# A decoder step in split fp32: first sums on GpSimd, norms in column groups inside the scans, the last norm's tiles regrouped

## The chip, the core and the metric

The kernel runs on one core of one Trainium2 chip. The metric is the device time of one execution in microseconds, the median of several runs. The engines are TensorE (PE in the profile; its weight loads PEld), VectorE (DVE), ScalarE (ACT), GpSimd (POOL) and SyncE (SP, which issues most DMAs). Each works through its own list in order and waits for the others by semaphores.

## What is computed

One inference step of a hybrid decoder layer, for a prompt of 16 + 1024 tokens and 8 decode samples, width 1024, in fp32:

```
h += 0.5 * swiglu(rmsnorm(h, n1), w1g, w1u, w1d)          # FFN1, inner width 2816
u  = rmsnorm(h, nm) @ w_in                                # q, f, v, g of 4 HGRN2 heads; z, x, B, C, dt of Mamba-2
# HGRN2 head:  S_t = diag(f_t) S_{t-1} + k_t v_t^T,  o_t = S_t^T q_t;  rmsnorm(o) * hg_norm * silu(g)
# Mamba-2:     h_t = exp(dt A) h_{t-1} + dt x B^T,   y = h C + D x;    grouped rmsnorm(y * silu(z)) * ssm_norm
h += concat(hgrn_out, ssm_out) @ w_out
h += 0.5 * swiglu(rmsnorm(h, n2), w2g, w2u, w2d)          # FFN2
y  = rmsnorm(h, norm_final)
```

The outputs are y for prompt and samples and the new recurrent states.

## The kernel before

Channels lie on the 128 partitions, tokens along the free axis: 1048 tokens (1032 after the scans, where the 16 meta tokens are dropped). A product of the large matrices is made in split precision: each operand is the sum of a high part (a cast, ScalarE) and a low part (a subtraction, VectorE), and three matmuls (lines 163, 164, 165) add up in one PSUM bank.

**FFNs.** Each pair of output blocks is made by seven block products in place of eight (Winograd's form of Strassen's scheme), whose operands are sums of blocks: of weights (`Left.sum_`, line 460; high part `hi` 464, low part `lo` 468) and of activations (`Blocks.sum_`, line 343; `cast` 348, `low` 354). `first1` is written for the first pair of FFN1: while the input arrives by DMA in token tiles, `x.place` transposes and scales them for the first pair of blocks, and `x.place_k` (lines 994 to 997) does the rest, channel block by channel block. `before(S, i, ...)` puts work ahead of step i of the product list. The order on TensorE, VectorE, ScalarE and SyncE is that of the code; the order on GpSimd is chosen by a scheduler. GpSimd builds masks at the start (lines 884 to 931) and does little else.

**Scans.** `ssm_scan` runs over nine chunks (the last has 16 tokens), then `hgrn_scan` four times, one head each. The projections that later heads need are cut into small steps; `fill(n)` issues n of them on TensorE between the small matmuls of a scan, so that TensorE has work while VectorE and ScalarE prepare the next level. `hgrn_scan` goes through levels m = 1, 2, 4, ... 64; at each it takes one of the `jobs` handed to it (the norm of the head before). At levels 1 and 32 `samples` loads four decode states by SyncE and updates them on ScalarE (line 1488) and VectorE (1489); after the levels eight one-column matmuls (line 1630), with the 128 x 128 states as weights, read them out. The norms (`hgrn_out`, line 1648, and `ssm_norm`, line 1396) square, sum over partitions by a matmul with a matrix of ones, which leaves the sum on all 128 partitions, and take the inverse root of 1032 columns in `rstd_wide` (ScalarE logarithm and exponential behind a table load, three VectorE steps, lines 203 to 205). The norm of Mamba group 0 runs between heads 0 and 1. Here only TensorE's order is that of the code.

**The end.** In the last `down` of FFN2, `Final` normalises 128 tokens at a time (transposes, line 1703; sum of squares; scale, line 1717), at given steps of the product list, and `LastFinal` takes the last 264 tokens as three tiles of 88 in three parts: transposes at line 1729, ScalarE squares (1735) and VectorE multiplications by the norm's weights (1736). Line 763 adds each finished product to the residual and frees its PSUM bank.

Of the kernel before, what the change touches and what calls it, by code (L numbers as in the profile page):

```python
# [12 lines left out]
AF = mybir.ActivationFunctionType  # L13
# [10 lines left out]
NS = 8  # L24
# [165 lines left out]
def rstd_wide(K, v, r, after):  # L190

    nc = K.nc
    with K.tc.issue_after(after.ins):
        ld = nc.scalar.preload_act_table_set("natural_log_exp_and_others")
    with K.tc.issue_after(ld.ins):
        n = v.shape[1] // 2
        parts = [(v[:, s : s + n], r[:, s : s + n]) for s in (0, n)]
        for vp, rp in parts:
            nc.scalar.activation(rp, vp, AF.Ln)
        for vp, rp in parts:  # L200
            nc.scalar.activation(rp, rp, AF.Exp, scale=-0.5, bias=K.lna)
    return [
        lambda: nc.vector.tensor_mul(v, v, r),
        lambda: nc.vector.scalar_tensor_tensor(v, v, -1.0, r, ALU.mult, ALU.mult),
        lambda: nc.vector.scalar_tensor_tensor(r, v, 3.0 * 2.0 ** (-2.0 / 3.0), r, ALU.add, ALU.mult),
    ]
# [112 lines left out]
class Blocks:  # L319
# [19 lines left out]
    def sum_(self, p):  # L339
        x, y = {5: (7, 1), 6: (3, 5), 7: (3, 7), 4: (2, 6)}[p]  # L340
        x, y = self.b[x], self.b[y]
        t = self.b[p] if p == 7 else self.new(p)
        self.K.nc.vector.tensor_sub(t, x, y)  # L343
# [99 lines left out]
class Left:  # L443
# [12 lines left out]
    def sum_(self, p):  # L456
# [3 lines left out]
        self.K.nc.vector.tensor_tensor(self.raw[p], self.raw[x], self.raw[y], op)  # L460
# [737 lines left out]
def ssm_scan(K, a, o, fill):  # L1198
# [45 lines left out]
    def back(c, hT):  # L1244
# [4 lines left out]
        if c > 0:  # L1249
# [3 lines left out]
            nc.vector.tensor_mul(ec[:, :, :n], pi.rearrange("p (j t) -> p j t", j=4)[:, :, :n], ec[:, :, :n])  # L1253
        py = K.psm()
# [3 lines left out]
        pyv = py.rearrange("p (j t) -> p j t", j=4)  # L1258
        ps = K.psm()
# [124 lines left out]
def ssm_norm(K, g, tag, fill):  # L1384
# [7 lines left out]
    fill(10)  # L1392
    for c0, w in CHUNKS_O:
        cs = slice(c0 - NM, c0 - NM + w)
        ps = K.psm()[:, :w]
        nc.tensor.matmul(ps, K.ones[1], v[:, cs], start=True, stop=True)
# [720 lines left out]
```

## Time and profile before

| | |
|---|---|
| median of 3 runs | 1979.36 us (1977.38 to 1979.84) |
| the profiled execution: its own time, its span | 1983.28 us, 1981.5 us |
| mean granted TensorE clock | 0.991 |
| TensorE, VectorE, ScalarE, GpSimd busy | 98%, 73%, 42%, 4% |
| the largest lines | 163, 164, 165 (split products): 1310.8, 1300.4, 1297.5 us, overlapping |
| DMA | 258.45 MB, mean 130 GB/s |

The span runs from the first to the last instruction; times on the trace count from its start. Busy times of TensorE's lines overlap, since matmuls are pipelined. The stages lie about so: start 0 to 60 us, FFN1 to 850, projections and scans to 1240, output projection and FFN2 to the end.

### The profile page before, as it was taken

The page shows a single profiled execution, that of the slowest core. Times are in us where ns is not written, and L with a number is a line of the kernel's source. Part 1 is how long each engine was busy: PE and PEld are TensorE (multiplying, and loading weights), DVE is VectorE, ACT ScalarE, POOL GpSimd, SP SyncE. Part 2 cuts the span into 40 slices and gives each one's busy share as a digit, 9 for nine tenths or more (in the row PEclk, how much of TensorE's full clock was granted, in tenths as well). Part 3 has the DMA queues.
Part 4 walks back from the last instruction along what each step waited for, and adds up shares of the span by engine and source line. Part 5 has one row for each costly group of instructions (what it writes and reads, how often), then busy time and mean ns, then how long its engine had stood idle before and what let it go on. Part 6 is the DMA issues. An engine that isn't in the chain of part 4 may idle for free.

```text
span 1981.5 us, 40896 instructions
## 1 busy us (share of the span) xinstructions
PE 1937.6 (98%) x16687; PEld 1900.4 (96%) x16687; DVE 1455.1 (73%) x2515; ACT 835.4 (42%) x1587; POOL 85.7 (4%) x135
## 2 busy tenths in 40 slices
PE   7999999999999999999999999999999999999997
PEld 6999999999999999998989999999999999999997
DVE  7777777778688776575665567987777777768974
ACT  7522222224534655465544445742222222354352
POOL 4000000000000410000000002200000000000000
PEclk9999999999999999999999999999999999999999
DMA  7233242335976542232442254224232423487851
GB/s 219 78 100 98 82 129 82 112 83 155 295 246 223 175 133 60 55 102 63 131 121 67 78 167 141 71 87 117 85 109 81 127 83 113 152 245 237 270 179 67
DMA packets 323876, 258.45 MB, mean 130 GB/s; under 512 B 17568, under 2 KB 299424, under 8 KB 323680
## 3 DMA queue, kind: packets, MB, share of 16 engines
q1 hardware_dynamic: 323448, 255.79, 42.6%
q8 instruction: 132, 2.16, 0.5%
q14 instruction: 56, 0.46, 0.1%
q0 software_dynamic: 224, 0.04, 0.0%
q10 hardware_dynamic: 16, 0.00, 0.0%
HBM read 190.79 MB, written 65.05 MB: 129 GB/s over the span
## 4 chain that ended last, share of the span: by engine, by line
PE 84%; DVE 9%; DMA 2%; issue 2%; ACT 2%; SPq 0%; POOL 0%; DVEq 0%; ACTq 0%; POOLq 0%
PE acc L163 26%; PE acc L165 26%; PE acc L164 26%; DVE u L354 1%; DVE ws L468 1%; PE mis L1540 1%; DMA r<-in_w_ffn_up_dram 1%; DMA u<-hd 1%; DVE u L677 1%; DVE ws L739 1%; DVE u L343 0%; PE mis L1261 0%; DVE r L460 0%; PE mis L1600 0%; DVE t L548 0%
## 5 line engine op out<-in xcount | busy, mean ns | idle before, releaser
L163 PE MATMUL acc<-u,ws 128*128 128x258 f32 (+4 forms) x4482 | 1310.8, 293 | 8.4 <-DVE t L562 2.7
L164 PE MATMUL acc<-u,ws 128*128 128x258 f32 (+4 forms) x4482 | 1300.4, 290 | 3.3 <-DVE u L354 1.8
L165 PE MATMUL acc<-u,ws 128*128 128x258 f32 (+4 forms) x4482 | 1297.5, 290 | 3.4 <-DVE ws L468 3.3
L163 PEld LDWEIGHTS acc<-u,ws 128*128 128x128 f32 x4482 | 849.2, 190 | 13.6 <-issue 5.1
L164 PEld LDWEIGHTS acc<-u,ws 128*128 128x128 f32 x4482 | 851.6, 190 | 6.1 <-DVE u L354 2.8
L165 PEld LDWEIGHTS acc<-u,ws 128*128 128x128 f32 x4482 | 849.0, 189 | 5.3 <-DVE ws L468 4.9
L468 DVE TENSOR_TENSOR ws<-r,ws 128x512 fp32r<-128x512 f32 x308 | 212.8, 692 | 78.8 <-ACT ws L464 78.8
L464 ACT CAST ws<-r 128x512 fp32r<-128x512 f32 x308 | 173.8, 615 | 5.0 <-DVE r L460 4.8
L583 ACT ACTIVATE t<-t 128x524 f32<-128x524 f32 (+1 forms) x47 | 29.9, 640 | 299.6 <-DVE t L548 299.6
L460 DVE TENSOR_TENSOR r<-r,r 128x512 f32<-128x512 f32 x176 | 121.1, 690 | 8.3 <-DMA r<-in_w_ffn_up_dram 6.5
L560 ACT ACTIVATE t<-t 128x516 f32<-128x516 f32 (+1 forms) x41 | 26.2, 639 | 200.3 <-DVE t L548 200.3
L677 DVE TENSOR_TENSOR u<-u,u 128x1048 fp32r<-128x1048 f32 (+3 forms) x84 | 97.2, 1159 | 10.2 <-ACT u L673 9.4
L232 POOL TENSOR_TENSOR t<-t,t 128x262 f32<-128x262 f32 (+1 forms) x56 | 57.5, 1036 | 814.9 <-ACT t L231 811.8
L548 DVE TENSOR_TENSOR t<-t,u 128x524 f32<-128x524 f32 (+1 forms) x135 | 90.4, 698 | 2.8
L158 DVE TENSOR_TENSOR ws<-r,ws 128x512 fp32r<-128x512 f32 x88 | 60.9, 702 | 40.0 <-ACT ws L157 39.5
L734 ACT CAST ws<-u 128x512 fp32r<-128x512 f32 (+1 forms) x72 | 42.1, 585 | 99.9 <-DVE u L729 91.6
L673 ACT CAST u<-u 128x1048 fp32r<-128x1048 f32 (+3 forms) x84 | 82.8, 988 | 1.3 <-DMA u<-hd 1.3
L763 DVE SCALAR_TENSOR_TENSOR s<-acc,s 128x524 f32<-128x524 f32 (+3 forms) x86 | 53.8, 649 | 33.8 <-PE acc L165 33.5
L739 DVE TENSOR_TENSOR ws<-r,ws 128x512 fp32r<-128x512 f32 (+1 forms) x84 | 56.3, 681 | 29.8 <-ACT ws L734 29.5
L734 ACT CAST ws<-r 128x512 fp32r<-128x512 f32 (+1 forms) x84 | 47.5, 582 | 65.9 <-DVE r L729 39.7
L553 ACT COPY t<-acc 128x524 f32<-128x524 f32 (+3 forms) x46 | 26.4, 574 | 103.5 <-PE acc L165 103.5
L157 ACT CAST ws<-r 128x512 fp32r<-128x512 f32 x88 | 53.6, 617 | 34.5 <-PE acc L165 31.1
(393 smaller groups left out, 1875.2 us busy)
## 6 DMA issues: line engine op xcount, KB each, us to landing
r<-in_w_ffn_down_dram SPq DMA_DIRECT2D x128, 256.0 KB
hd<-s SPq DMA_DIRECT2D x93, 258.0 KB
r<-in_w_ffn_gate_dram SPq DMA_DIRECT2D x88, 256.0 KB
r<-in_w_ffn_up_dram SPq DMA_DIRECT2D x88, 256.0 KB
hd<-s SPq DMA_DIRECT2D x77, 262.0 KB
u<-hd SPq DMA_DIRECT2D x36, 516.0 KB
u<-hd SPq DMA_DIRECT2D x28, 524.0 KB
r<-in_w_in_dram SPq DMA_DIRECT2D x56, 256.0 KB
```

Of the source, the lines that this page charges most:

```text
L158: self.nc.vector.tensor_sub(lo, src, hi.bitcast(F32))
L163: mm(ps, whi, xhi, start=first, stop=False, skip_group_check=more)
L164: mm(ps, whi, xlo, start=False, stop=False, skip_group_check=more)
L165: mm(ps, wlo, xhi, start=False, stop=last, skip_group_check=more)
L460: self.K.nc.vector.tensor_tensor(self.raw[p], self.raw[x], self.raw[y], op)
L464: self.K.nc.scalar.copy(self.w[p][:, : self.n * P], self.raw[p])
L468: self.K.nc.vector.tensor_sub(t[:, 512 : 512 + w], self.raw[p], t[:, :w].bitcast(F32))
L548: nc.vector.tensor_mul(t, t if src is None else src, spread.lanes(i, cs))
L673: K.nc.scalar.copy(hi, lo.bitcast(F32))
L677: K.nc.vector.tensor_sub(lo, lo.bitcast(F32), hi.bitcast(F32))
L734: nc.scalar.copy(w[p, j, g][:, : n * P], src)
L739: nc.vector.tensor_sub(t[:, 512 : 512 + n * P], box[0], t[:, : n * P].bitcast(F32))
```

## The change

The order rows below are an engine's instructions in program order, with output, input and shape and what is waited for; numbers tell buffers of one name apart.

**First pair of FFN1.** The four sums of weights (products 5, 6, 7, 3) and three of the sums of operands (5, 6, 4 of the second half) are issued on GpSimd. The low parts of product 1 stand ahead of input tile 3. On GpSimd the sums (L478 of weights, L361 of operands; the lines of after stand 18 further down here) come behind the masks:

```order
L914 AFFINE_SELECT mf_8712<-ones_83 128x64 [waits Pool_49]
L915 AFFINE_SELECT mf_8712<-mf_8712 128x64 [waits Pool_49]
L918 CAST mask_8715<-mf_8712 32x16 [waits Pool_49]
L918 CAST mask_8715<-mf_8712 32x16 x3
L478 TENSOR_TENSOR r_239<-r_147,r_149 128x512 [waits DMAHW2_49,DMAHW1_49,Pool_49]
L478 TENSOR_TENSOR r_241<-r_239,r_139 128x512 [waits DMAHW5_49,Pool_49]
L478 TENSOR_TENSOR r_147<-r_139,r_147 128x512
L478 TENSOR_TENSOR r_244<-r_145,r_241 128x512 [waits DMAHW0_49,Pool_49]
L361 TENSOR_TENSOR u_468<-u_328,u_324 128x1048 [waits DVE_49]
```

The seven sums are new there; before, L232 (now L250) followed the last mask. On ScalarE this is the place of product 5 before (L464 is the cast of a sum of weights, L996 and L997 copy a placed input tile out of PSUM):

```order
L553 COPY t_297<-acc_284 128x262 [waits PE_49]
L348 CAST u_299<-u_282 128x1048 [waits DVE_49]
L464 CAST ws_303<-r_301 128x512 [waits DVE_49]
L996 ACTIVATE u_319<-mis_314,col_100 128x262 [waits PE_49]
L997 COPY u_321<-mis_314 128x262
L996 ACTIVATE u_323<-mis_314,col_100 128x250
L997 COPY u_325<-mis_314 128x250
L557 COPY t_339<-acc_284 128x262 [waits PE_49]
```

and now, with L482 as that cast and L1014 and L1015 as the copies:

```order
L571 COPY t_304<-acc_291 128x262 [waits PE_49]
L366 CAST u_306<-u_289 128x1048 [waits DVE_49]
L482 CAST ws_308<-r_239 128x512 [waits Pool_49]
L1014 ACTIVATE u_324<-mis_319,col_100 128x262 [waits PE_49]
L1015 COPY u_326<-mis_319 128x262
L1014 ACTIVATE u_328<-mis_319,col_100 128x250
L1015 COPY u_330<-mis_319 128x250
L575 COPY t_344<-acc_291 128x262 [waits PE_49]
```

The rows are the same; the cast now waits for GpSimd, and the copies stand behind it as they did.

**Scans.** Two `fill(2)` stand between the small matmuls of Mamba's last chunk. `rstd_wide` becomes `Rms`: four matmuls with 32 columns of ones put the sums of a quarter of the tokens each on 32 partitions, so that root and steps work on 258 columns; `part(i)` brings a quarter back to 128 partitions by a matmul with one row. The norm of group 0 becomes a list of jobs inside head 1's scan. Decode states are loaded at levels 1 and 8 and updated at 4 and 64; their readout has 32 columns of weights, mostly zeros, with the states as moving operand, then a ScalarE copy and two four-column matmuls. On TensorE, the end of group 0's norm and the start of head 1 before (L163 to L165 are projection steps, L1396 the norm, L1465 the transposes of head 1):

```order
L163 MATMUL acc_11867<-u_8344,ws_11525 128x344
L164 MATMUL acc_11867<-u_8352,ws_11525 128x344
L165 MATMUL acc_11867<-u_8344,ws_11525 128x344
L1396 MATMUL mis_11883<-s_11846,ones_83 128x344 [waits DVE_49,PE_49]
L1396 MATMUL mis_11886<-s_11846,ones_83 128x344
L1396 MATMUL mis_11889<-s_11846,ones_83 128x344
L163 MATMUL acc_11867<-u_8345,ws_11525 128x344
...
L163 MATMUL acc_11926<-u_8340,ws_11802 128x350 [waits Activation_49]
L164 MATMUL acc_11926<-u_8348,ws_11802 128x350
L165 MATMUL acc_11926<-u_8340,ws_11802 128x350
L1465 MATMUL mis_11933<-ident,u_11067 128x128 x4
```

and the same norm now (L1541 and L1570 are products of head 1's first two levels, L203 the matmuls of `root`):

```order
L164 MATMUL acc_11856<-u_8351,ws_11504 128x344
L165 MATMUL acc_11856<-u_8343,ws_11504 128x344
L1541 MATMUL mis_11904<-u_10571,u_10726 32x32 [waits DVE_49]
L1541 MATMUL mis_11904<-u_10571,u_10726 32x32 x31
L1542 MATMUL mis_11903<-u_10571,u_10726 16x16 [waits Activation_49]
L1570 MATMUL mis_11938<-s_11899,u_10726 32x16 [waits DVE_49,Activation_49]
L1570 MATMUL mis_11938<-s_11899,u_10726 32x16 x31
L1582 MATMUL mis_11903<-s_11899,u_10726 16x8
L203 MATMUL mis_11984<-s_11841,ones_83 32x258 [waits Activation_49]
L203 MATMUL mis_11984<-s_11841,ones_83 32x258 x3
L163 MATMUL acc_11856<-u_8344,ws_11509 128x344
```

The norm's matmuls moved from ahead of head 1 to behind its second level, and there are four of 258 columns for three of 344.

**The end.** The last three `Final`s run at steps closer together, one with banks of the accumulators' pool; `LastFinal` has tiles of 128, 128 and 8 tokens, its first multiplications go to a ScalarE copy and GpSimd, and the second part's square is one instruction of 384 columns into a tile of its own.

```diff
-def rstd_wide(K, v, r, after):
...
+class Rms:
...
+    def root(self):
+        K, w = self.K, self.w
+        nc = K.nc
+        ps = K.psm()[:, :w]
+        for i in range(4):
+            nc.tensor.matmul(ps[32 * i : 32 * i + 32], K.ones[1][:, :32], self.v[:, i * w : i * w + w], start=True, stop=True)
+        self.r, self.q = K.t(w), K.t(w)
+        an = nc.scalar.activation(self.q, ps, AF.Identity, scale=self.scale, bias=K.eps)
+        with K.tc.issue_after(an.ins):
+            ld = nc.scalar.preload_act_table_set("natural_log_exp_and_others")
+        with K.tc.issue_after(ld.ins):
+            nc.scalar.activation(self.r, self.q, AF.Ln)
+            nc.scalar.activation(self.r, self.r, AF.Exp, scale=-0.5, bias=K.lna)
+    def newton(self):
+        nc, q, r = self.K.nc, self.q, self.r
+        nc.vector.tensor_mul(q, q, r)
+        nc.vector.scalar_tensor_tensor(q, q, -1.0, r, ALU.mult, ALU.mult)
+        nc.vector.scalar_tensor_tensor(r, q, 3.0 * 2.0 ** (-2.0 / 3.0), r, ALU.add, ALU.mult)
+    def part(self, i):
+        K, w = self.K, self.w
+        ps = K.psm()[:, :w]
+        K.nc.tensor.matmul(ps, K.ones[1][32 * i : 32 * i + 1], self.r[32 * i : 32 * i + 1], start=True, stop=True)
+        return ps, slice(i * w, i * w + w)
...
-    def sum_(self, p):
+    def sum_(self, p, pool=False):
...
-        self.K.nc.vector.tensor_sub(t, x, y)
+        (self.K.nc.gpsimd if pool else self.K.nc.vector).tensor_sub(t, x, y)
...
-        self.K.nc.vector.tensor_tensor(self.raw[p], self.raw[x], self.raw[y], op)
+        (self.K.nc.gpsimd if pool else self.K.nc.vector).tensor_tensor(self.raw[p], self.raw[x], self.raw[y], op)
...
+        if n < P:
+            fill(2)
         py = K.psm()
...
         pyv = py.rearrange("p (j t) -> p j t", j=4)
+        if n < P:
+            fill(2)
         ps = K.psm()
...
-    fill(10)
-    for c0, w in CHUNKS_O:
-        cs = slice(c0 - NM, c0 - NM + w)
-        ps = K.psm()[:, :w]
-        nc.tensor.matmul(ps, K.ones[1], v[:, cs], start=True, stop=True)
-        an = nc.scalar.activation(v[:, cs], ps, AF.Identity, scale=1.0 / 256, bias=K.eps)
-    for step in rstd_wide(K, v, r, an):
-        step()
-    for i, y in enumerate((ya, yb)):
+    rms = Rms(K, v, 1.0 / 256)
+    def spread(i):
+        ps, cs = rms.part(i)
+        nc.scalar.copy(r[:, cs], ps)
+    def scale(i, y):
         nc.vector.scalar_tensor_tensor(y, y, K.pc["ssm_norm"][:, 2 * g + i : 2 * g + i + 1], r, ALU.mult, ALU.mult)
+    def end():
+        scale(1, yb)
+        then()
+    return [rms.root, lambda: None, rms.newton, lambda: (spread(0), spread(1)), lambda: (spread(2), spread(3)), lambda: scale(0, ya), end]
...
-        if m in (1, 32):
-            samples({1: 0, 32: 4}[m])
+        if m in (1, 8):
+            samples_load({1: 0, 8: 4}[m])
         if jobs:
             jobs.pop(0)()
             fill(2)
+        if m in (4, 64):
+            samples({4: 0, 64: 4}[m])
...
+    qz = K.t(32 * NS).rearrange("p (b i) -> p b i", b=NS)
+    nc.gpsimd.memset(qz, 0.0)
+    nc.scalar.copy(qz[:, :, 0], qs[:, :NS])
     fill(6)
+    pr = K.psm()
+    for b in range(NS):
+        nc.tensor.matmul(pr[32 * (b % 4) : 32 * (b % 4) + 32, b // 4 * P : b // 4 * P + P], qz[:, b], states[b // 4 * 4][:, b % 4], start=True, stop=True)
+    rows = K.t(2 * P)
+    nc.scalar.copy(rows, pr[:, : 2 * P])
+    fill(1)
...
-    for b in range(NS):
-        nc.tensor.matmul(po8[:, 16 + b : 17 + b], states[b // 4 * 4][:, b % 4], qs[:, b : b + 1], start=True, stop=True)
+    for i in range(2):
+        nc.tensor.matmul(po8[:, 16 + 4 * i : 20 + 4 * i], rows[:, i * P : i * P + P], K.ident[:, 0:P:32], start=True, stop=True)
...
+    def gate(i):
+        ps, cs = rms.part(i)
+        nc.vector.tensor_mul(g[:, cs], g[:, cs], ps)
+    def end():
+        gate(3)
         then()
-    jobs = [root, None, None, None, gate]
-    return [lambda i=i: jobs[i]() for i in range(5)]
+    return [rms.root, lambda: None, rms.newton, lambda: (gate(0), gate(1)), lambda: (gate(2), end())]
...
-            ps = K.psm()
+            ps = self.bank()
...
+        self.tiles = [(t0 + c, min(P, n - c)) for c in range(0, n, P)]
...
+            K.nc.scalar.activation(yt[:n, 512:], ps[:n], AF.Square, accum_out=self.st[:n, 0, j : j + 1])
+            K.nc.scalar.copy(yt[:n, :512], ps[:n])
+            K.nc.gpsimd.tensor_mul(yt[:n, :512], yt[:n, :512], self.nf[0][:n, :512])
...
+            K.nc.scalar.activation(junk[:n], ps[:n, : 3 * P], AF.Square, accum_out=st[:n, 1, j : j + 1])
+            for c0, c1, f0 in ((0, 256, 512), (256, 384, 896)):
+                K.nc.vector.tensor_mul(yt[:n, f0 : f0 + c1 - c0], ps[:n, c0:c1], self.nf[0][:n, f0 : f0 + c1 - c0])
...
+        o.low(1)
+        w.lo(1)
+        for p in (5, 6, 7, 3):
+            w.sum_(p, True)
         scaled, raw3 = x.place(3)
         K.keep_clock(4)
         scaled(0)
-        o.low(1)
         scaled(1)
-        w.lo(1)
         w.hi(2)
...
-        before(S, 1, (o.cast, 5), (w.sum_, 5), (w.hi, 5), (o.sum_, 6), (x.store, 0), (columns,), (x.place_k, 0))
-        before(S, 2, (o.low, 5), (o.cast, 6), (w.lo, 5), (w.sum_, 6), (w.hi, 6), (x.place_k, 1))
-        before(S, 3, (o.low, 6), (o.sum_, 7), (w.lo, 6), (o.cast, 7), (w.sum_, 7), (w.sum_, 3), (w.hi, 7), (x.place_k, 2))
+        before(S, 1, (o.cast, 5), (w.hi, 5), (o.sum_, 6), (x.store, 0), (columns,), (x.place_k, 0))
+        before(S, 2, (o.low, 5), (o.cast, 6), (w.lo, 5), (w.hi, 6), (x.place_k, 1))
+        before(S, 3, (o.low, 6), (o.sum_, 7), (w.lo, 6), (o.cast, 7), (w.hi, 7), (x.place_k, 2))
...
+        before(S, 5, (o.low, 3), (w.lo, 3), (e.cast, 1), (e.sum_, 5, True), (x.store, 1, (0,)), (x.place_k, 4), (x.place_k, 5))
...
+        before(S, 7, (e.cast, 2), (e.low, 5), (e.low, 2), (e.sum_, 6, True), (x.store, 1, (1,)), (o.cast, 4), (e.cast, 6))
...
+        before(S, 9, (e.sum_, 4, True), (e.low, 7), (e.cast, 3), (x.square, 9))
...
-                    fill(5)
+                    fill(4)
                     fn()
                 outs = []
                 fill.until("z0")
-                fill(10)
-                ssm_norm(K, 0, "s", fill)
-                for i in range(2):
-                    spill(2 + i, K.y[i][:, NM:])
+                fill(4)
+                outs = ssm_norm(K, 0, "s", lambda: [spill(2 + i, K.y[i][:, NM:]) for i in range(2)])
...
-        ssm_norm(K, 1, "s", fill)
+        fill(4)
+        for fn in ssm_norm(K, 1, "s", lambda: None):
+            fill(3)
+            fn()
...
-        for t0, at in ((3 * P, e3 + 6), (6 * P + 8, e3 + 11), (7 * P + 8, e3 + 16), (0, e0 + 1), (P, e0 + 3), (2 * P, e0 + 5)):
-            f = Final(K, o, h, nf, t0)
-            S.before(at, f.begin)
-            S.before(at + 2, f.root)
-            S.before(at + 3, f.end)
-        last = LastFinal(K, o, h, nf, 4 * P, 88)
+        for t0, bank, at in (
+            (3 * P, K.psm, (e3 + 6, e3 + 8, e3 + 9)),
+            (6 * P + 8, K.psm, (e3 + 11, e3 + 13, e3 + 14)),
+            (7 * P + 8, K.psm, (e3 + 16, e3 + 18, e3 + 19)),
+            (0, K.psm, (e0 + 1, e0 + 2, e0 + 3)),
+            (P, K.psum, (e0 + 2, e0 + 3, e0 + 4)),
+            (2 * P, K.psm, (e0 + 5, e0 + 6, e0 + 7)),
+        ):
+            f = Final(K, o, h, nf, t0, bank)
+            for i, fn in zip(at, (f.begin, f.root, f.end)):
+                S.before(i, fn)
+        last = LastFinal(K, o, h, nf, 4 * P, 2 * P + 8)
```

More of the change, by code (lines that the diff above doesn't have):

```diff
@@ L187, in rstd, with __init__ @@
         return newton
-def rstd_wide(K, v, r, after):
[L192 to L206, printed above, removed]
+class Rms:
+    def __init__(self, K, v, scale):
+        self.K, self.v, self.scale = K, v, scale
+        self.w = v.shape[1] // 4
+    def root(self):
[21 more added lines that the diff above has]
+        return ps, slice(i * w, i * w + w)
 class Norm:
@@ L1485, in samples @@
         nc.sync.dma_start(vb, vd[b0 : b0 + 4].partition_broadcast(P))
+        states[b0] = sb, vb
+    def samples(b0):
+        sb, vb = states[b0]
         for i in range(4):
```

71 lines of the change are left out of this document (29 added, 42 removed).

## The prediction

> **What bounds the kernel now.** I read the page first, then the busy time by stage (stretches cut where the work changes), then who waited for whom in the stretches with idle time, then single rows there.
>
> ```profile
> span 1981.5 us, 40896 instructions
> PE 1937.6 (98%) x16687; PEld 1900.4 (96%) x16687; DVE 1455.1 (73%) x2515; ACT 835.4 (42%) x1587; POOL 85.7 (4%) x135
> core 0: us, PE busy (x) PEld busy (x) DVE busy (x) ACT busy (x) POOL busy (x), PEclk, DMA share, GB/s
> 14.00:30.00 16.00, 10.72 (x78) 9.02 (x77) 15.24 (x22) 13.69 (x31) 8.00 (x12) 1.00 1.02 294
> 30.00:60.00 30.00, 24.97 (x164) 22.86 (x164) 24.92 (x33) 25.75 (x52) 0.00 (x0) 0.89 0.30 97
> 905.00:950.00 45.00, 41.97 (x652) 39.13 (x651) 24.65 (x71) 19.91 (x44) 1.83 (x4) 0.92 0.36 96
> 950.00:1200.00 250.00, 245.87 (x2780) 231.68 (x2779) 146.64 (x356) 129.88 (x266) 3.90 (x10) 0.97 0.37 110
> 1940.00:1981.00 41.00, 28.19 (x237) 27.36 (x235) 16.89 (x59) 10.87 (x38) 0.00 (x0) 0.90 0.18 66
> ```
>
> TensorE is busy for 1937.6 of 1981.5 us; all other engines have room over the whole span. So time can be won in three ways only: TensorE idle time, stretches where its clock is below 1.00, and the work after its last matmul. The five stages quoted hold what the change touches: idle 5.3 us in 14–30, 5.0 in 30–60, 3.0 in 905–950, 4.1 in 950–1200, 12.8 at the end. In 14–30 VectorE is the full engine (15.24 of 16) and ScalarE nearly so (13.69).
>
> The profiled run took 1983.28 us (span 1981.5 and 1.8 around it), 3.9 above the median of the runs, 1979.36. I work out differences on this span and take them off the median. About 0.2%, 4 us, is what a measurement of this kernel can tell from no change.
>
> **Part 1, the first pair of FFN1.** Seven sums go from VectorE to GpSimd: four of weights (128x512), three of operands (128x1048).
>
> ```profile
> L460 DVE TENSOR_TENSOR r<-r,r 128x512 f32<-128x512 f32 x176 | 121.1, 690 | 8.3 <-DMA r<-in_w_ffn_up_dram 6.5
> 33.58 1.25 DVE L343 TENSOR_TENSOR u<-u,u 128x1048 f32<-128x1048 f32 x1
> 691.03 0.75 POOL L232 TENSOR_TENSOR t<-t,t 128x262 f32<-128x262 f32 x1 [3.03 <-ACT t L231]
> 678.28 5.04 POOL L232 TENSOR_TENSOR t<-t,t 128x262 f32<-128x262 f32 x2 [4.37 <-ACT t L231]
> 18.97 3.58 POOL L900 CAST mask<-mf 32x16 uint8<-32x16 f32 x4
> 19.16 0.62 ACT L464 CAST ws<-r 128x512 fp32r<-128x512 f32 x1
> PE acc L165 <- DVE ws L468: 2.6, 4, 1.3
> PE mis L164 <- DVE u L354: 2.1, 3, 0.8
> PE mis L994 <- DMA s<-in_x_prompt_dram: 2.0, 2, 1.0
> PE acc L164 <- DVE u L354: 1.8, 3, 0.9
> ```
>
> VectorE loses 4 x 0.69 + 3 x 1.25 = 6.5 us. GpSimd has no sum of these sizes in the trace. Its nearest row takes 0.75 us for 262 columns; by columns that is at most 1.5 for 512 and 3.0 for 1048; I take 1.3 and 2.5, since part of 0.75 will be fixed. That holds beside a quiet VectorE; beside a full one two such instructions of 262 columns took 5.04, so 2.5 each or more.
>
> The queue matters more. GpSimd works in order and builds masks until 18.97 + 3.58 = 22.55 us; the first sum stands behind them. The ScalarE cast of that sum (product 5, line 464) now starts at 19.16; after the change it waits for GpSimd until some 22.7, about 3 us later, and the four copies of a placed input tile, which release TensorE, are queued behind it. The other three sums follow at 1.3 each, faster than ScalarE asks for them. So one delay of about 3 us, then a VectorE that has 6.5 us less to do, in a stretch where TensorE waits 2.6 + 2.1 + 1.8 us for VectorE's low parts. I let this recover 2.5. The low parts moved ahead of tile 3 gain nothing: TensorE then waits for the tile's DMA (2.0) anyway. The three operand sums, at 2.5 each or more beside a full VectorE, hold it and the low parts up by 1 to 4; I take 2. Start: **+2.5 us**, with -4 (sums hidden, VectorE's relief passed on) and +6 as ends. From 60 us on TensorE is nearly never idle, so this shift stays.
>
> The Trainium skill, "GPSIMD Engine Reference", 4.1 Engine selection, puts two-input elementwise work on VectorE, GpSimd being about twice as slow, and section 1 says that the two share their SBUF interfaces when VectorE has two SBUF inputs. Here GpSimd takes 0.75 for 262 columns and VectorE 0.69 for 512, 2.1 times, and 5.04 for two beside a full VectorE, so the trace agrees; without the rule's second half the start would be the -4 above.
>
> **Part 2, the scans.** Here the loss is idle time and half clock.
>
> ```profile
> 911.42:914.83 3.41, 3.41 (x12) 3.23 (x12) 0.81 (x2) 0.00 (x0) 0.21 (x1) 0.50 0.00 0
> 942.14:945.56 3.42, 3.42 (x14) 3.42 (x12) 3.23 (x8) 1.66 (x5) 0.00 (x0) 0.50 0.56 140
> 972.86:976.28 3.42, 3.42 (x14) 3.42 (x14) 2.26 (x13) 1.57 (x8) 0.00 (x0) 0.50 0.62 185
> 1024.06:1030.89 6.83, 5.94 (x101) 5.56 (x105) 6.67 (x10) 2.40 (x6) 0.00 (x0) 0.50 0.58 198
> 1184.49:1187.90 3.41, 3.41 (x10) 2.47 (x10) 1.50 (x3) 1.86 (x4) 0.00 (x0) 0.50 0.96 359
> PE mis L1540 <- issue: 2.7, 2, 1.6
> PE mis L1512 <- ACT s L1466: 1.5, 1, 1.5
> PE mis L1540 <- DVE s L1501: 1.3, 1, 1.3
> 933.40 0.94 DVE L1489 SCALAR_TENSOR_TENSOR r<-r,qs,r 128x128 f32<-128x128 f32 x3 [2.65 <-ACT r L1488]
> 970.82 1.93 PE L1630 MATMUL mis<-qs,r 128*128 128x1 f32 x16
> 1014.93 1.90 PE L1396 MATMUL mis<-s,ones 128*128 128x344 f32 x6
> 1021.15 1.23 DVE L203 TENSOR_TENSOR s<-s,s 128x1032 f32<-128x1032 f32 x1 [12.51 <-ACT s L201]
> L1511 PE MATMUL mis<-u,u 128*32 128x32 f32 x256 | 3.1, 199 | 0.0
> ```
>
> Six windows of 3.41 us run at 0.50 (the two from 1024.06 together 6.83). Each costs at most 1.7 when TensorE is full. They stand right behind sparse TensorE work: the last chunk's tiny matmuls (911), sixteen one-column matmuls from 970.82 (972), the same in head 3 (1184), the norm's two stalls (1024). The change takes away or fills each of these; the one at 942 follows the stalls inside head 0, which it changes only by the way. Taking back 0.8 to 0.85 of 1.7 for 911, 972 and 1184, 0.85 of 2.9 for the pair, half for 942, **-7.6**; ends 0 and -10.
>
> Stalls: the norm of group 0 stands alone between heads now, its VectorE steps of 1.23 on 1032 columns ahead of head 1's first products, and TensorE waits 1.5 + 1.3. After the change it is a list run inside head 1, with steps on 258 columns; I take 2.5 of the 2.8 back. The 2.7 of "issue" inside head 0 lie in dense groups of small matmuls that stay. What changes beside them are the decode samples: VectorE stands 2.65 us there behind ScalarE, which waits for samples whose load was issued in the same step. Loads now go out two or three steps ahead of their use, the second pair earlier than before in SyncE's queue, where nothing else is due; its store leaves later, which nothing waits for. That, with the fill around it, takes 2.3 off, 1 to 2.5. Stalls together **-4.8**, ends -1.5 and -6.5.
>
> Work: the sixteen passes of 1.93 us per head become sixteen with 32 columns of weights in four column groups, and four short ones (each matmul shows as two passes). Groups of 32 columns do run beside one another: the 256 passes of line 1511 are busy 3.1 us, 12 ns each, though one lasts 199. I take 0.8 off per head, **-3.1**; +1.8 if they run one behind another. Each of the six norms had six passes in 1.90; now four in column groups (two passes of 258 columns, 2 x 1.90 / 6 x 258 / 344 = 0.48) and four one-row matmuls that spread the result back, which the trace does not show: 0.48 each is 1.9, and 1.0 if two run at a time. That is -0.4 to +0.5 for each norm, and +1.9 if not even the groups overlap, so -2.5 to +11 for six; I take **+1.3**, since the root's overlap has line 1511's row behind it and the spreading has none. Middle: -7.6 - 4.8 - 3.1 + 1.3 = **-14**, range -8 to -19 (not all bad ends at once).
>
> The Trainium skill, "TensorE: Matmul & The Clock Gate", Part 1, drops the clock to half after an idle window of about 3.4 us. The window length fits the rows; an idle gap of that length stands before none of the six, the longest here is 1.6. Taken literally the rule blames something other than these places, and they would come back: the third rival.
>
> **Part 3, the end.**
>
> ```profile
> PE acc L1729 <- DVE s L763: 3.4, 2, 1.8
> out_dram<-u SPq DMA_DIRECT2D x3, 352.0 KB
> 1963.22 1.41 DVE L1717 SCALAR_TENSOR_TENSOR u<-mis,ssq,u 128x512 f32<-128x512 f32 x2
> 1964.55 0.42 DVE L763 SCALAR_TENSOR_TENSOR s<-acc,s 128x258 f32<-128x258 f32 x1
> 1970.02 0.41 DVE L763 SCALAR_TENSOR_TENSOR s<-acc,s 128x258 f32<-128x258 f32 x1
> 1960.50:1961.00 0.50, 0.50 (x7) 0.50 (x6) 0.50 (x1) 0.50 (x3) 0.00 (x0) 1.00 1.01 410
> 1977.00:1978.00 1.00, 0.00 (x0) 0.00 (x0) 0.00 (x0) 0.00 (x0) 0.00 (x0) 0.50 0.70 270
> ```
>
> Twice the transposes of the last tokens wait for VectorE (3.4 us), which reaches the sum of line 763 only at 1964.55 and 1970.02, behind normalising rows (1.41 for two) and multiplications. The change pulls three finals forward by one or two products, gives the first multiplications to ScalarE and GpSimd, and halves the ping-pong between ScalarE and VectorE on the same tile. I take 2.9 of 3.4. One final now takes its banks from the accumulators' pool, where a bank comes free with a sum of 0.42; I cost that at nothing, and at 1 us if that sum is late. The last stores, 3 x 352 KB from 88 partitions, move at 270 GB/s, while a store of 128 rows moves at 410; two of 128 rows and one of 8 end 1056 KB / 270 - 1056 KB / 410 = 1.3 earlier, and the first of them leaves earlier in the row too; I take 2.1. End: **-5**, range -2.5 to -6.5. If the cover fails (a longer square of 384 columns, the wait for GpSimd), the 3.4 stay and -2.5 is left.
>
> Sum: +2.5 - 14 - 5 = -16.5, so 1979.36 - 16.5 = **1963 us** (and a profiled run like the one here at 1966.8).
>
> **The rivals.** (a) GpSimd's sums are hidden. For: from 14 to 30 VectorE is the engine without room. Against: the masks end at 22.55. Start -3.5 in place of +2.5: **1957**, chance 0.2. (b) The shared interface takes over: GpSimd gets on only between VectorE's instructions, ScalarE's queue stands behind each sum and TensorE behind ScalarE. For: 5.04 for two. Against: there VectorE was not relieved. The loss is the seven sums' time, less 6.5, plus the 3 at the queue. From 26.5 us in all, 3.8 each, it eats the 19 of the other parts and 4 more. At 5 each it is 31.5 and the kernel ends at 1979.4 + 12.5 = **1992**, slower; chance 0.04. (c) The half-clock windows move and do not go: -16.5 + 7.6 = -8.9, **1970.5**; for it, the sparse groups of line 1540 that stay, and four one-row matmuls in a row are sparse too; chance 0.2. (d) The new matmul forms don't overlap: middle 4.9 + 9.7 worse at the most, **1977.6** at that end; against it line 1511's 12 ns; chance 0.06.
>
> **How the numbers follow.** The forecast has 0.5; its own terms span 1957 to 1969. The range must leave out no more than 0.2: with (a) and (c) in it and the ends of the start, **1953 to 1974**; out are (b), the end of (d), and the joint best ends. Within 0.2% (over 1975.4) come the end of (d) and a mild (b), 0.07; slower 0.03; faster 0.9.
>
> **What would show it.** Right: the cast of product 5 on ScalarE waits for GpSimd until about 22.7; TensorE reaches its state of 60 us some 2 to 3 us later; no granted 0.50 at the places of 911, 972, 1024 and 1184; TensorE idle in 950–1200 under 2; no wait for line 763's successor at the end, and the last store's data gone within 4 us of its issue. Wrong: GpSimd sums of 128x512 above 2.5 us or under 0.9, windows of 0.50 as many as now, or new waits of head 1's products for the norm's list.

## The result, and the profile after

The changed kernel takes 1967.36 us (median of 4 runs, 1966.59 to 1968.4), the kernel before 1979.6 beside it (1977.38 to 1981.57): 12.2 us less, a ratio of 0.9945 with a 95% interval of 0.9932 to 0.9958. The forecast was 1963, range 1953 to 1974. The profiled execution took 1967.93 us, its span is 1965.9.

The busy time by stage of the changed kernel (columns: start and end, length, busy time of PE, PEld, DVE, ACT and POOL with counts, granted clock, DMA share, GB/s) answers to the stages shown of before; the last one is cut 10 us earlier.

```profile
14.00:30.00 16.00, 9.48 (x55) 7.80 (x55) 11.23 (x14) 9.04 (x22) 12.73 (x19) 0.89 0.91 279
30.00:60.00 30.00, 23.32 (x135) 21.08 (x136) 22.79 (x25) 23.96 (x48) 8.94 (x3) 0.77 0.24 81
905.00:950.00 45.00, 44.34 (x654) 40.80 (x654) 28.48 (x79) 26.38 (x55) 2.42 (x4) 1.00 0.29 74
950.00:1200.00 250.00, 249.11 (x3016) 232.14 (x3006) 151.96 (x395) 131.64 (x275) 4.85 (x13) 1.00 0.40 119
1930.00:1965.00 35.00, 27.43 (x231) 26.86 (x229) 14.87 (x55) 11.96 (x35) 3.77 (x3) 0.91 0.20 77
```

The first two rows got worse: 55 matmuls in 14–30 where there were 78, 135 in 30–60 for 164, and a granted clock of 0.89 for 1.00 and 0.77 for 0.89. The two rows of the scans got better: TensorE idle 0.7 for 3.0 and 0.9 for 4.1, the clock at 1.00.

How far a kernel is can be read without any cut, since the 4624 passes of the split products' first matmul (line 163) are the same in every kernel here. The time at which the same pass starts, kernel minus before, from the two profiles:

```
pass    before, us   after minus before   place
  64       59.37          +7.5            second pair of FFN1
2140      906.19          +9.2            ahead of the last chunk of the Mamba scan
2640     1234.59          -9.7            scans over, output projection
4400     1878.48         -10.9            last products of FFN2
 end     1981.47         -15.6            end of the span
```

So the start lost 7.5, FFN1 another 1.8, the scans gave 19.0, FFN2 1.1 and the end 4.7. (Before's profiled run lay 3.7 above the median of its runs, the changed kernel's 0.6: 15.6 on the traces is 12.2 on the medians.)

The start: who waited for whom on TensorE in 0 to 60 us, then GpSimd's, ScalarE's and VectorE's rows (start, duration, instruction, and in brackets the idle time before it and who ended it).

```profile
PE acc L164 <- DVE u L372: 5.2, 5, 2.3
PE acc L163 <- ACT ws L482: 1.1, 1, 1.1
...
21.00 0.89 POOL L918 CAST mask<-mf 32x16 uint8<-32x16 f32 x4
21.98 5.55 POOL L478 TENSOR_TENSOR r<-r,r 128x512 f32<-128x512 f32 x4
35.90 2.42 POOL L361 TENSOR_TENSOR u<-u,u 128x1048 f32<-128x1048 f32 x1 [8.37 <-DVE u L999]
...
23.27 0.62 ACT L482 CAST ws<-r 128x512 fp32r<-128x512 f32 x1 [4.27 <-POOL r L478]
...
46.32 3.81 DVE L372 TENSOR_TENSOR u<-u,u 128x1048 fp32r<-128x1048 f32 x2 [0.73 <-ACT u L366]
51.21 4.63 DVE L372 TENSOR_TENSOR u<-u,u 128x1048 fp32r<-128x1048 f32 x2
```

The masks end at 21.89, the first sum comes behind them, and ScalarE has stood 4.27 us when the cast of product 5 begins at 23.27 (19.16 before). Each sum of 512 columns takes 5.55 / 4 = 1.39 us, one of 1048 takes 2.42. Where a sum of 1048 runs beside VectorE's low parts, two of these take 3.81 and 4.63 in place of 2.5.

The scans: all waits of TensorE from 905 to 1200 us, then the new matmuls (groups by line: count, busy us, mean ns of one).

```profile
PE mis L1570 <- issue: 0.7, 1, 0.7
PE mis L223 <- DVE t L217: 0.4, 1, 0.4
PE mis L203 <- ACT s L1418: 0.4, 1, 0.4
...
L223 PE MATMUL mis<-t,ones 1*128 1x258 f32 x48 | 7.1, 426 | 0.5 <-DVE t L217 0.4
L203 PE MATMUL mis<-s,ones 128*32 128x258 f32 x40 | 3.2, 391 | 0.0
L1650 PE MATMUL mis<-r,t 128*32 128x128 f32 x64 | 2.6, 279 | 0.0
L1671 PE MATMUL mis<-ident,t 128*128 128x4 f32 x16 | 2.3, 252 | 0.0
```

1.5 us of waits are left of 7.0 in the same stretch of before, and no window of 0.50 lies between 54 us and the last matmul. Four heads' readout costs 2.6 + 2.3 = 4.9 for 4 x 1.93 = 7.7. A norm's root costs 8 x 3.2 / 40 = 0.64 and its spreading 7.1 / 6 = 1.18, together 1.8 for 1.90.

The end: one wait of 0.6 is left for the residual sum (line 781, 763 before), and the last stores move at 418 GB/s.

```profile
PE acc L1769 <- DVE s L781: 0.6, 1, 0.6
...
1961.00:1962.00 1.00, 0.00 (x0) 0.00 (x0) 0.53 (x3) 0.31 (x1) 0.00 (x0) 0.50 1.03 418
```

### The profile page after: what moved, and what is told of

It reads as the page before. It is cut to its first block, busy times and chain, and to the rows that moved or that the text cites. A ratio compares the mean times of both kernels' runs of the same rounds, so it can differ in the third digit from the quotient of the medians.

```text
span 1965.9 us, 41084 instructions
## 1 busy us (share of the span) xinstructions
PE 1929.7 (98%) x16763; PEld 1889.9 (96%) x16763; DVE 1441.4 (73%) x2516; ACT 831.0 (42%) x1580; POOL 101.8 (5%) x151
## 4 chain that ended last, share of the span: by engine, by line
PE 85%; DVE 10%; issue 2%; ACT 2%; POOL 1%; DMA 1%; SPq 0%; ACTq 0%; DVEq 0%; POOLq 0%
PE acc L163 26%; PE acc L165 26%; PE acc L164 26%; DVE u L372 1%; DVE u L695 1%; DVE ws L757 1%; DVE s L781 1%; PE mis L1570 1%; DVE r L747 1%; DVE s L724 1%; DVE ws L486 1%; PE mis L1283 0%; DVE u L747 0%; PE mis L1632 0%; PE mis L1277 0%
## 5 line engine op out<-in xcount | busy, mean ns | idle before, releaser
L163 PE MATMUL acc<-u,ws 128*128 128x258 f32 (+4 forms) x4482 | 1309.3, 292 | 8.3 <-DVE t L580 2.1
L165 PE MATMUL acc<-u,ws 128*128 128x258 f32 (+4 forms) x4482 | 1298.0, 290 | 3.2 <-DVE ws L486 3.1
L163 PEld LDWEIGHTS acc<-u,ws 128*128 128x128 f32 x4482 | 847.9, 189 | 19.2 <-issue 10.1
L165 PEld LDWEIGHTS acc<-u,ws 128*128 128x128 f32 x4482 | 847.4, 189 | 4.9 <-DVE ws L486 4.5
L482 ACT CAST ws<-r 128x512 fp32r<-128x512 f32 x308 | 173.8, 615 | 9.3 <-DVE r L478 4.5
L478 DVE TENSOR_TENSOR r<-r,r 128x512 f32<-128x512 f32 x172 | 118.4, 690 | 7.8 <-DMA r<-in_w_ffn_up_dram 6.0
L250 POOL TENSOR_TENSOR t<-t,t 128x262 f32<-128x262 f32 (+1 forms) x56 | 54.5, 983 | 774.2 <-ACT t L249 771.0
L757 DVE TENSOR_TENSOR ws<-u,ws 128x512 fp32r<-128x512 f32 (+1 forms) x72 | 47.4, 658 | 26.5 <-ACT ws L752 26.5
```

What stands on the lines that cost most here:

```text
L163: mm(ps, whi, xhi, start=first, stop=False, skip_group_check=more)
L165: mm(ps, wlo, xhi, start=False, stop=last, skip_group_check=more)
L478: (self.K.nc.gpsimd if pool else self.K.nc.vector).tensor_tensor(self.raw[p], self.raw[x], self.raw[y], op)
L482: self.K.nc.scalar.copy(self.w[p][:, : self.n * P], self.raw[p])
L757: nc.vector.tensor_sub(t[:, 512 : 512 + n * P], box[0], t[:, : n * P].bitcast(F32))
```

## The experiments

The kernel before ran beside each group: 1978.87, 1979.77 and 1979.61 us. The place table of all of them, from the profiles, stands at the end of this section.

### The start: what the sums on GpSimd cost

**All seven back on VectorE**, all else as changed:

```diff
-        for p in (5, 6, 7, 3):
-            w.sum_(p, True)
...
+        before(S, 1, (o.cast, 5), (w.sum_, 5), (w.hi, 5), ...
...
-        before(S, 5, ..., (e.sum_, 5, True), ...
+        before(S, 5, ..., (e.sum_, 5), ...
```

> The changed kernel with the seven sums on VectorE again, in their old steps, and the low parts of product 1 in their old place; all else as changed. Theory Q (the queue: the first sum stands behind the masks on GpSimd, ScalarE's cast behind the sum, TensorE behind ScalarE) and theory S (the shared SBUF interface: the sums are slow and stretch VectorE's own instructions) both expect the 7.5 us back that TensorE is late at 67 us: about 1960 us, 1967.4 less 7.5. If the loss at the start comes from something else, 1967.

Measured: 1960.94 us, ratio 0.9906 (0.9892 to 0.9921). Leaving the sums where they were is worth 6.4 us over the change, on the medians of the whole kernel, and 6.0 on the profiles at pass 64. TensorE's work up to that pass, in this kernel and in the changed one:

```profile
0.00:60.84 60.84, 47.74 (x309) 43.51 (x309) 46.86 (x71) 46.56 (x93) 20.28 (x53) 0.92 0.61 188
0.00:66.84 66.84, 49.81 (x308) 44.67 (x309) 46.83 (x65) 46.90 (x93) 34.05 (x60) 0.87 0.54 171
```

Of the 6.0, 3.9 are idle time (17.0 for 13.1) and 2.1 the same matmuls at a lower clock (five half-clock windows for three). The start is where the changed kernel loses, and the sums are why. The edit also puts product 1's low parts back; the kernel with only the sums of operands on GpSimd, below, keeps them ahead of tile 3 and is 1.3 late at pass 16, where this one is 0.8 late and the kernels with an unchanged start lie between 0 and 2.5, so their place shows no price.

**Only the sums of weights on GpSimd** (the three of operands with `False`):

> Of the sums only the four of weights stay on GpSimd, the three of operands go back to VectorE. Theory Q: the cast of product 5 still waits until about 23 us, some 6 of the 7.5 us stay, about 1966 us. Theory S: the larger instructions were the costly ones (VectorE's low parts of 1.24 us took 1.9 and 2.3 beside them), half or more comes back, 1963 us or less.

Measured: 1966.7 us, 0.9933 (0.9915 to 0.9951); TensorE 6.0 late at pass 64, 4.5 more than with all seven on VectorE. On the profile it is as theory Q had it; the interval of the time reaches down to theory S's 1963.

**Only the sums of operands on GpSimd:**

> The other half: the four sums of weights on VectorE in their old steps, the three of operands on GpSimd, product 1's low parts ahead of tile 3 as in the change. Theory Q: no wait of ScalarE for GpSimd before 30 us, TensorE 1 to 2 us late at 67 us against the kernel before, about 1961.5 us. Theory S: TensorE 4 us late or more, 1964 us or more.

Measured: 1965.33 us, 0.9929 (0.9914 to 0.9945); TensorE 3.7 late at pass 64, 2.2 more than with all on VectorE. It lies between the two: later than theory Q had it, and ScalarE waits for no sum of weights; earlier at the start than theory S had it, with a median inside theory S's bound. The two halves make 4.5 + 2.2 = 6.7, near the 6.0 of both.

**Masks behind the fourth sum of weights:**

```diff
-    K.tri = cst.tile([P, P], F32, name="tri")
...
+    with K.tc.issue_after(K.last_sum.ins):
+        K.tri = cst.tile([P, P], F32, name="tri")
...
```

> The changed kernel with the masks built behind the fourth sum of weights on GpSimd; every sum stays there. Theory Q: the first sum runs before 17 us, the cast of product 5 is where it was before the change (about 19), and 4 to 6 of the 7.5 us come back: 1961 to 1963.5 us. Theory S: the sums wait between VectorE's instructions, over 2 us each where they took 1.39; the cast starts after 21 and less than 2 us come back: over 1965 us.

Measured: 1968.74 us, 0.9944 (0.9929 to 0.9959): nothing came back, where theory Q expected 4 to 6. Its profile, GpSimd, ScalarE, VectorE and TensorE's largest wait:

```profile
13.17 7.44 POOL L478 TENSOR_TENSOR r<-r,r 128x512 f32<-128x512 f32 x4 [6.99 <-DMA r<-in_w_ffn_up_dram]
36.98 2.81 POOL L921 CAST mask<-mf 32x16 uint8<-32x16 f32 x4
39.88 2.39 POOL L361 TENSOR_TENSOR u<-u,u 128x1048 f32<-128x1048 f32 x1
...
20.47 0.61 ACT L484 CAST ws<-r 128x512 fp32r<-128x512 f32 x1
...
17.16 4.55 DVE L361 TENSOR_TENSOR u<-u,u 128x1048 f32<-128x1048 f32 x2
...
PE acc L163 <- ACT u L366: 7.2, 1, 7.2
```

The sums start at 13.17 and the cast no longer waits for them; at pass 16 TensorE is 1.2 late where the changed kernel is 6.3. But the masks now fill GpSimd until 39.79, the first operand sum stands behind them, and TensorE waits 7.2 us for the cast of that. The queue's price moved from the weights' sums to the operands'.

**Masks behind all seven sums** (the same edit, with the last operand sum as the one to follow):

> The changed kernel with the masks behind all seven sums on GpSimd, so that none of the sums has anything ahead of it. Theory Q (queue) in its stricter form, that each sum behind the masks pays for them: neither the 6 us at product 5 nor the 6.7 us that moved to the first operand sum with the masks between; TensorE is then late at 67 us only by what the slower sums themselves cost, 2 us more than with the sums on VectorE, about 1963 us. Theory S (shared interface): the four sums of weights stretch VectorE's instructions from 13 us on and the operand sums theirs, 5 us or more late, 1966 us or more. If GpSimd's relief of VectorE pays after all, under 1960.

Measured: 1965.24 us, 0.9926 (0.9906 to 0.9946); 3.9 late at pass 64, 3.5 less than the change and 2.5 more than all on VectorE. With both queues gone the rest, 2.5, is put down to the slower sums themselves. At pass 64 theory Q holds for the larger part, and the interface that theory S names is the smaller. The whole kernel's time does not show this split: of the 6.4 us only 2.1 came back on the medians, with intervals that overlap, and 1965.24 lies nearer to theory S's 1966 than to theory Q's 1963. From pass 64 to 2140 this profile loses another 2.0, 1.5 of it in one half-clock window near 771. The sums of weights show the interface too: here four take 7.46 beside VectorE, 1.87 each for 1.39, and VectorE's own sum of two at 17.4 takes 4.56 for 2.5.

### The scans: whose were the 19 us

**The norms alone**, added to the kernel before:

> The kernel before with only the norms of the change (root on 258 columns, spreading by one-row matmuls, group 0's norm as jobs in head 1's scan). Theory P (each place owns its loss): the two half-clock windows behind group 0's norm and the 2.8 us of waits there go, the windows near 911, 942 and 973 stay; 7 to 9 us less, about 1971. Theory F (the half-clock windows fall where their free-running phase happens to meet a thin stretch): as many windows as before, at other places; 3 to 4 us less, 1975.5.

Measured: 1982.4 us, 1.0006 (0.9992 to 1.0020): no gain at all, against both theories. Behind group 0's norm 6.2 us are won as expected (passes 2280 to 2340), and 8.4 are lost earlier, at head 0's norm (passes 2200 to 2260). There ScalarE shows:

```profile
977.28 1.28 ACT L208 ACT_TABLE_LOAD   x1
978.58 0.42 ACT L210 ACTIVATE t<-t 128x258 f32<-128x258 f32 x1
979.02 1.28 ACT L1439 ACT_TABLE_LOAD   x1
980.31 0.46 ACT L1439 ACTIVATE u<-acc 128x344 f32<-128x344 f32 x1
980.79 1.28 ACT L211 ACT_TABLE_LOAD   x1
982.08 0.51 ACT L211 ACTIVATE t<-t,lna 128x258 f32<-128x258 f32 x1
...
985.78 1.14 PE L223 MATMUL mis<-t,ones 1*128 1x258 f32 x4 [3.21 <-DVE t L217]
```

Between the logarithm (line 210) and the exponential (211) the scheduler put a projection's activation, which needs another table: two loads of 1.28 more, TensorE waits 3.21 and three half-clock windows of 3.41 follow. In the changed kernel, with the rest of the change in place, the order of the work on ScalarE falls otherwise at this head, and no table comes between; which part of the rest does that no run separates. As to the other windows, the pair at group 0's norm is gone, as theory P had it; of the four others as many are left, as theory F had it: those of 942 and 1184 are missing, and two stand at 1071 and 1126, behind the sixteen one-column passes of heads 1 and 2, where the kernel before had none.

**The same with two halves of 129 columns** in each root, so that there is always a next piece of the same table (the kernel before worked its roots in two halves, and the change dropped that):

```diff
-            nc.scalar.activation(self.r, self.q, AF.Ln)
-            nc.scalar.activation(self.r, self.r, AF.Exp, scale=-0.5, bias=K.lna)
+            parts = [(self.q[:, s : s + w // 2], self.r[:, s : s + w // 2]) for s in (0, w // 2)]
+            for qp, rp in parts:
+                nc.scalar.activation(rp, qp, AF.Ln)
+            for qp, rp in parts:
+                nc.scalar.activation(rp, rp, AF.Exp, scale=-0.5, bias=K.lna)
```

> The kernel before with only the norms of the change, as in the run of the norms alone (1982), and in each root the logarithm and the exponential on two halves of 129 columns, so that ScalarE's scheduler has no gap to put a table of another function between. Theory T (ScalarE's order: a projection's activation came between the logarithm and the exponential of head 0's norm, two more table loads of 1.28, TensorE 3.2 late and two half-clock windows behind it): the wait of 3.2 and those two windows go, 5 to 7 us less than the norms alone, about 1976. Rival N (head 0's norm is late for its own longer chain: root, spread, gate): no more than 1.5 less, 1981.

Measured: 1976.25 us, 0.9988 (0.9978 to 0.9998). The wait of 3.2 and the windows behind it are gone from the profile: passes 2200 to 2260 cost 0.5 more than before, where the norms alone cost 8.4. On the medians it is 6.2 less than the norms alone, by the ratios 3.6, with intervals that just overlap; the profile decides for theory T.

**The samples alone:**

> The kernel before with only the decode samples of the change (loads two or three levels ahead, readout with 32 columns of weights). Theory P: the waits for nothing shown inside head 0 (2.7) and the window near 942 go with the late loads, the windows near 973 and 1184 with the sixteen one-column passes; the windows at 911 and behind group 0's norm stay; 8 to 10 us less, about 1970. Rival G (those waits belong to the dense groups of small matmuls themselves): they stay, with the window near 942; 4 us less, 1975.

Measured: 1974.26 us, 0.9979 (0.9966 to 0.9993). TensorE has no wait left from 905 to 950 us, so in this profile the waits for nothing shown went with the samples, against rival G; windows of 0.50 are at 914 and 1020 only. But they do not always go: two kernels with the same samples, those with only the sums of weights on GpSimd and with the masks behind all sums, wait 1.5 and 1.8 for "issue" there, and the first has a window at 939. Nor does the missing window near 942 prove the samples' part, since three of the five profiles without them have none there either. The profile gives 10.6 for the scans, the medians 5.5.

**The two fills alone:**

> The kernel before with only the two fills in Mamba's last chunk. Theory P (that place owns its half-clock window): no window between 905 and 920, 1 to 1.5 us less there, which the run's time can hardly show, 1978.5. Theory F (free-running phase): a window of 0.50 there or right behind, or a new one elsewhere.

Measured: 1979.93 us, 0.9998 (0.9989 to 1.0008). The window at 911 is gone (1.25 won from pass 2140 to 2160), and so is that of 942; five are left in the scans, one of them new at 1067. All five profiles without the fills have the window of 911 and none of the nine with them does: the place owns it, and one place cannot be seen in the run's time.

**Group 0's norm between the heads**, narrow as it is, in the kernel with the sums back:

```diff
-                outs = ssm_norm(K, 0, "s", lambda: [spill(...) for i in range(2)])
+                for fn in ssm_norm(K, 0, "s", lambda: [spill(...) for i in range(2)]):
+                    fill(3)
+                    fn()
+                outs = []
```

> The changed kernel with the seven sums on VectorE, and group 0's norm not inside head 1's scan but between the heads, its steps on 258 columns with three projection steps ahead of each. Theory V (the place counts: the norm's chain behind head 1's own preparation keeps TensorE waiting): 2 us or more of waits come back and a half-clock window with them, 1963.5 to 1965. Theory W (the width counts: steps of 0.43 in place of 1.23): within 1 us of 1961.

Measured: 1964.93 us, 0.9917 (0.9902 to 0.9932), 4.0 more than 1960.94 with intervals that overlap. In that place the profile has this wait again:

```profile
PE mis L203 <- DVE s L1413: 1.5, 1, 1.5
```

and from pass 2280 to 2340 it wins 6.0 where the norm inside head 1 wins 7.5. Theory V as to the direction; no half-clock window came back.

So whose were they? From pass 2140 to 2640 the profiles give -10.6 for the samples, -3.4 for the fills (1.25 of it at their own place), +0.4 for the norms and -9.4 for the norms with halves, against -19.0 for the whole change and +0.7 for the kernel with only the end changed, whose scans are those of before. Windows that move make up differences of some 2 us between such profiles.

### The end, and the best version

**The end alone:**

> The kernel before with only the end of the change (finals closer together, last tiles of 128, 128 and 8 tokens). If the end stands by itself, the two waits of 3.4 us for the residual sum fall to 0.6 and the last stores run at 400 GB/s and more; 4.5 to 5 us less than before, about 1974.5.

Measured: 1974.66 us, 0.9975 (0.9964 to 0.9987), 5.0 from pass 4400 to the end on the profile. The end stands by itself.

**Sums back and halves in the roots:**

> The changed kernel with the seven sums on VectorE (1961) and the halves of 129 columns in each root. Theory T: in that kernel two roots (group 0's and head 1's) still have a table between, but TensorE waits only 0.4 there; 0 to 1 us less, 1960 to 1961. If VectorE's or TensorE's work behind those tables was late without showing a wait, 2 us or more less, 1959 or under.

Measured: 1959.72 us, 0.9894 (0.9879 to 0.9909): the fastest kernel here, 7.6 us below the change, between theory T's 1960 and the other reading's 1959; its lead of 1.2 over the sums back alone lies within their intervals.

The places, kernel minus before in us, from one profile each (the kernels with an unchanged start differ there by 1.9 among themselves, so much is the noise of one profile):

```
kernel                      pass 64   2140    2640    4400    end
changed                       7.5     9.2    -9.7   -10.9   -15.6
sums back                     1.5     0.9   -17.9   -18.8   -23.6
weight sums on GpSimd         6.0     6.1   -10.5   -11.9   -16.7
operand sums on GpSimd        3.7     4.7   -14.6   -15.5   -20.2
masks behind weight sums      7.9    11.3    -8.0    -9.7   -14.4
masks behind all sums         3.9     5.9   -12.1   -12.6   -17.3
norms alone                   0.8     2.3     2.7     3.1     3.4
norms alone, halves           0.4     0.7    -8.7    -7.9    -6.9
samples alone                 1.2     1.6    -9.0    -9.6    -9.5
fills alone                   1.4     2.2    -1.2    -2.5    -2.1
end alone                     2.0     3.4     4.1     2.3    -2.7
norm between heads            0.2     1.5   -13.7   -14.9   -19.8
sums back, halves             0.9     1.2   -18.4   -18.4   -23.2
```

## Why the prediction came out as it did

The sign and the three parts held; two sizes were off in opposite directions, the scans by 5.0 and the start by 3.5 to 5.0. That they nearly cancel is luck: on the profiles 15.6 us went where 16.5 were forecast, on the medians 12.2.

**The start: +2.5 forecast, +6.0 measured** at pass 64 against the kernel with the sums back, 7.5 against the kernel before. The queue was found rightly: the sums at 21.98 for 22.55, 1.39 and 2.42 us for 1.3 and 2.5, and the cast at 23.27. But "some 22.7, about 3 us later" left out the first sum's own time: by the prediction's rows 22.55 + 1.3 = 23.85, 4.7 later. It came 4.1 later, because the masks ended 0.66 earlier; their last four casts took 0.89 beside an idle VectorE where they had taken 3.58. The step that failed is "I let this recover 2.5". Nothing was recovered: the cast came 4.1 late, and TensorE was 6.3 late at pass 16. The sums of weights cost 4.5 at pass 64 where 3 - 2.5 = 0.5 was forecast. VectorE's 6.5 us of relief fell where it was waiting (busy 11.23 of 16 in 14–30), not where TensorE waited for it. That the low parts beside the later sums were stretched (1.22 for 0.68 at 23.92, 2.19 for 1.24 at 26.45) and that a thinned-out TensorE got more half-clock windows belongs to the same loss (the 3.9 of idle time and 2.1 of clock above); how much each caused no run tells. The 2 us for the operand sums were right: 2.2 and 2.5, though single profiles of one start differ by 1.9. Rival (a) is refuted; rival (b) is there, but with a price of 2 to 3 us at pass 64 and not 31; its ground, 5.04 for two, was taken beside a VectorE that was busy for 3.72 of them and not full.

**FFN1: no term, +1.8 measured.** The four kernels with operand sums on GpSimd lose 1.0 to 3.4 from pass 64 to 2140, the others -0.5 to 1.5. A half-clock window near 770 us, worth 1.5, stands in six of the profiles, four of them without operand sums on GpSimd; without it the ranges are 0.5 to 1.9 and -0.7 to 0.4. The cause is not settled.

**The scans: -14 forecast, -19.0 measured.** Waits fell by 7.0 - 1.5 = 5.5 (forecast 4.8; of the 7.0, 2.7 + 1.5 + 1.3 were counted, 1.5 lay in smaller ones). The readout saved 2.8 (3.1). The norms' matmuls cost 6 x 0.08 = 0.5 less (1.3 more was forecast): the root's four groups overlap, and the one-row matmuls do so in part, 1.18 for four where 1.9 was the price of none and 1.0 of pairs. What is left, 19.0 - 5.5 - 2.8 - 0.5 = 10.2, is the six windows within 0.4: TensorE was busy in them for 3.41 + 3.42 + 3.42 + 5.94 + 3.41 = 19.6 us at half clock, 9.8 more than at full clock. The term of 7.6 was too small because it gave back 15 to 50% of each as if other windows would come, and none did. Rival (c) is refuted for the change as a whole: of the seven kernels with all of the scans' changes six have no window there, one has one at 939. In the kernels with a part of the change windows do turn up in new places, 1067, 1071, 1114 and 1126; but the kernel with only the end changed, whose scans are those of before, has them at 1072 and 1126 too. Which of the thin places left get a window differs from profile to profile, and only with all of the scans' changes were they gone, but for the one at 939. Rival (d) is refuted: the new forms overlap, the spreading in part. The Trainium skill's rule ("TensorE: Matmul & The Clock Gate", Part 1), by which an idle window of about 3.4 us halves the clock, does not tell of these: no such idle time had stood before any of them, and they went with the thin stretches. The prediction put the 2.7 of "issue" down to the samples only in part; with the samples alone they were gone in the one profile, and 0.7 stayed in the changed kernel.

**The end: -5 forecast, -4.7 measured** (5.0 alone), and the waits and the store rate are as expected, 0.6 for 3.4 and 418 GB/s for 270.

What the forecast did not see at all is that the norms' gain depends on ScalarE's order, which decides whether a table comes between: alone, they gain nothing.

## What to carry to other kernels

Work moved to an idle engine costs what stands ahead of it in that engine's queue, besides its own duration: look up when the queue is empty, and what else queues behind the first consumer; moving the queue's other work back only helps if nothing later needs it. Relief of a full engine pays only if that engine was what the bound engine waited for at that moment. And pieces of one table's work should leave the scheduler no gap: in the kernel with the norms alone, one long dependent pair on ScalarE let in two more table loads of 1.28 us.

## What the runs showed of the hardware

- VectorE and GpSimd, both with two SBUF inputs, take turns by whole instructions: in the changed kernel a GpSimd sum runs from 50.27 to 53.57 us, and the VectorE low part that starts beside it at 51.21 takes 3.47 us, that is until 1.1 us behind the sum's end, the next one 1.24 again. Two low parts of 1.24 us so take 3.81 and 4.63 us beside one GpSimd sum, about their own time and part or most of that sum's; four sums of 512 columns take 7.46 in place of 5.55.
- In the scans of the kernel before, half-clock windows of 3.41 us come at or behind thin stretches in which TensorE was never idle for more than 1.6 us, and across the profiles not at each of them: of the four places with sixteen one-column passes, two or three had a window in each of the five profiles with those passes, not always the same, and none in the nine profiles without. In each profile all windows lie on one grid of 3.413 us (before: 911.42, 942.14, 972.86, 1024.06 and 1184.49 are 9, 9, 15 and 47 steps apart), and its offset differs between profiles. That the offset decides which thin place gets a window fits the rows; no run here tests it.
- One-row matmuls that spread 258 columns to 128 partitions take 148 ns a pass (7.1 us / 48), against 80 for the four-group root (3.2 / 40) and 317 for a pass of 344 columns before (1.90 / 6).
